# Moving the right operands' pool by 128 bytes and making the last projection's pool a multiple of 256 bytes, in a decoder block on one core

## The chip, the cores and the metric

The kernel runs on one core of one Trainium2 chip. The metric is the device time of one execution in microseconds (us), taken as the median of three runs. A separate execution was recorded by the hardware profiler; its views are quoted here as "the profile" or "the trace". The core has a matrix engine (PE, with its weight loads listed apart as PEld), a vector engine (DVE), a scalar engine (ACT), a general engine (POOL), an engine that mostly issues transfers (SP), and 16 DMA engines. On-chip memory has 128 partitions; an address here is a byte offset inside a partition, the same in all 128.

## The reference, cut to what matters

A residual block over 2048 tokens of width 1024:

```
h    = rms_norm(x, g) * (1 + scale) + shift            # scale, shift, gate from silu(c) @ w_mod
proj = h @ w_in                                        # 1024 x 8192: rnn x, rnn gate, q, k, v, attn gate, 2 merge gates
y_rnn  = (rg_lru(conv(x_rnn)) * silu(z_rnn)) @ w_out_rnn
y_attn = (dilated_attention(rope(q), rope(k), v) * silu(z_attn)) @ w_out_attn
merged = sigmoid(g_r + b) * y_rnn + sigmoid(g_a + b) * y_attn
x    = x + gate * (merged @ w_o);  out = rms_norm(x, g_final)
```

All matrix products keep float32 accuracy. The addresses at which operands lie do not enter the result.

## The kernel before, in words

Every float32 operand is split into a high part and a low part (`hi_act`, `lo_pool`, `lo_dve`, L157 to L168), and `mm3` (L152) makes one product out of three matmuls: high by high, high by low, low by high. Each matmul comes with its own weight load: the left operand (`lhsT`) is loaded into the array and stands, the right operand (`rhs`) moves through it, 512 columns or 256 at a time. The profile writes the result and then the two operands, so `X<-T,S` is a matmul into bank X whose operands lie in tiles T and S.

The stages, in order of time:

1. Values: `value_sums` and `value_runs` make v. Here a T tile (the normalised input, turned) is the standing operand, and an S tile (split weights, 256 columns) moves. For two of the four blocks of tokens half of T's part is held in `b12h` and `b12l` instead. With 4 weight groups, 4 blocks, 2 banks, 2 halves, 8 slices and 3 matmuls there are 1,536 such matmuls, 384 of them with b12.
2. The input projection, once for each half of the tokens. `strassen` (L362) makes 7 products where 8 would be plain; `prod` runs 4 slices times `mm3`, 12 matmuls of 512 columns for each product. Here S stands and T moves. There are 28 pairs of column tiles in each half, so 2 x 28 x 7 x 12 = 4,704 matmuls. Between products the recurrent branch puts in 32 groups of 6 matmuls (`gates` in `recurrent`), whose operands `xh`, `xl`, `gh`, `gl` lie in one pool.
3. Attention, whose operands all lie in one pool, with the two output projections (`steps`, results in pj) spread between its matmuls. Their moving operands `yh` and `yl` lie in pool `fl`, their standing ones in S0 to S3. The last two blocks of the second projection have their moving operand in F tiles: 192 matmuls with F against S0 to S3.
4. The last projection (`output_products`): eight pairs of token tiles, seven products each, 12 matmuls a product, F moving, S standing. Product i of each pair uses Si: B11 takes S0, T2 S1, T3 S2, T1 S3, B21 S4, T4 S5, B22 S6. PE runs them in the order S0, S6 of the pair before, S1, S2, S3, S4, S5.

The order of work inside each engine is written out by hand (`manual_schedule`) from L601 on.

Pools are laid out as two stacks in each partition. The left stack begins with pool `cp` (constants and small vectors, each tile rounded up to 32 bytes), and everything opened on the left lies behind it: `hp` with the 14 T slots, `vx` with b12, `rp` with xh, xl, gh, gl, `ap` with the attention's operands, and `fp` with the F slots. The right stack begins at the top end: `pS` with S0 to S3, `pR`, then `wS` and `wq` with S4 to S6, later `fl` with yh and yl, and for the last projection `gp`, which then holds S4 to S6.

In the program before, `cp` ends at byte 18,528 (72 x 256 + 96). A T or F slot has 8,192 bytes, a slice of it 2,048, so each of these operands starts at 96 modulo 256. S0 to S3 lie from 212,960 (831 x 256 + 224) on, in steps of 4,096 bytes, with slices of 512, so they start at 224 modulo 256; so do S4 to S6 in `wS`, and yh and yl in `fl`. Pool `gp` takes gf 4,096, three S 12,288, four xo 16,384, u1 to u3 8,192, four ss of 16 bytes rounded up to 32 (128), and two jk 2,048: 43,136 bytes, 168 x 256 + 128. It ends at 204,768, where `pR` begins, so it starts at 161,632, 96 modulo 256, and its S4 to S6 stand at 96 too. The pool of xh, xl, gh and gl puts them at 160, b12h and b12l are at 224, and cs (the identity for transposes, in `cp`) is at 128.

| operands (moving against standing) | before, modulo 256 | difference |
|---|---|---|
| T against S, input projection | 96, 224 | 128 |
| yh, yl against S0 to S3 | 224, 224 | 0 |
| F against S0 to S3 | 96, 224 | 128 |
| F against S4 to S6, last projection | 96, 96 | 0 |
| S against T, values | 224, 96 | 128 |
| S against b12, values | 224, 224 | 0 |
| xh, xl against gh, gl | 160, 160 | 0 |

Of the kernel before, what the change touches and what calls it, by code (L numbers as in the profile page):

```python
# [10 lines left out]
F32 = mybir.dt.float32  # L11
# [9 lines left out]
P = 128  # L21
# [68 lines left out]
def decoder_block(ctx, tc, x, c, positions, g_norm, w_mod, b_mod, w_in, b_gate, conv_w, conv_b,  # L90
                  w_a, b_a, w_x, b_x, lam, w_out_rnn, w_out_attn, w_o, g_final, cst, out):
    nc = tc.nc
    cnt = [0]

    def T(pool, shape, dt, tag, **kw):
        cnt[0] += 1
        return pool.tile(shape, dt, tag=tag, name=f"{tag}_{cnt[0]}", **kw)
# [26 lines left out]
    cp = ctx.enter_context(tc.tile_pool(name="cp", bufs=1))  # L124
# [20 lines left out]
    par = T(cp, [P, N_PAR], F32, "par")  # L145
    ones = T(cp, [P, 1], F32, "ones")
    nc.gpsimd.memset(ones[:], 1.0)

    def mm(o, l, r, st, sp, **kw):
        nc.tensor.matmul(o, lhsT=l, rhs=r, start=st, stop=sp, **kw)  # L150
# [1010 lines left out]
    for t in range(6):  # L1161
        pieces = []
        i0 = t * P
        while i0 < (t + 1) * P:
            hd, i = divmod(i0, 96)
# [777 lines left out]
    def output_products(fill):  # L1943
# [120 lines left out]
        def soon(d, fn):  # L2064
            i = max([e[1] for e in jobs], default=0) + 1
            jobs.append((done_n[0] + d, i, fn))
            jobs.sort(key=lambda e: e[:2])
# [24 lines left out]
        squares_of = {}  # L2092

        def first_root(ss):
            nc.vector.tensor_scalar(ss[:, 0], ss[:, 0], ss[:, 3], EPS, ALU.add, ALU.add)
            nc.scalar.activation(ss[:, 1], ss[:, 0], AF.Sqrt)

        def last_root(ss):
            v, y, t = (ss[:, i] for i in range(3))
            nc.vector.reciprocal(y, y)  # L2100
            nc.vector.tensor_scalar(t, y, y, v, ALU.mult, ALU.mult)
            nc.vector.tensor_scalar(t, t, -0.5, 1.5, ALU.mult, ALU.add)
            nc.vector.tensor_scalar(y, y, t, None, ALU.mult)

        def finish_last(x, i, j, ps):

            xo, cols = XO[x, i], slice(j * CH, (j + 1) * CH)
            tt(xo[:, cols], ps[:], xo[:, cols], ALU.add)
            whole = (x, i) in squares_of
            if not whole:  # L2110
                squares_of[x, i] = T(gp, [P, 4, 1], F32, "ss", bufs=4)
            ss = squares_of[x, i]
            jk = T(gp, [P, CH], BF16, "jk", bufs=2)
            nc.scalar.activation(jk[:], xo[:, cols], AF.Square, scale=D ** -0.5, accum_out=ss[:, 3 if whole else 0])
            if (i, j) == (0, 1):
                U[i, j] = T(gp, [P, CH], F32, "u1", bufs=1)[:]
                tt(U[i, j], xo[:, cols], gf[:, cols], ALU.mult)
            else:
                U[i, j] = xo[:, cols]
                nc.gpsimd.tensor_tensor(U[i, j], xo[:, cols], gf[:, cols], ALU.mult)  # L2120
            if whole:
                first_root(ss)
                last_root(ss)
                n, r = order[x]
                for q in (1 - j, j):
                    v = U[i, q]
                    if q == 1 - j:
                        nc.scalar.activation(v, v, AF.Copy, scale=ss[:, 1])
                    elif i:
                        nc.gpsimd.tensor_tensor(v, v, ss[:, 1].broadcast_to([P, CH]), ALU.mult)  # L2130
                    else:
                        nc.vector.tensor_scalar(v, v, ss[:, 1], None, ALU.mult)
                    nc.sync.dma_start(outv[n, r + i][:, q * CH : (q + 1) * CH], v)

        def finish(x, i, j, ps, u):

            if x == len(order) - 1:
                return finish_last(x, i, j, ps)
            xo, cols = XO[x, i], slice(j * CH, (j + 1) * CH)
            tt(xo[:, cols], ps[:], xo[:, cols], ALU.add)  # L2140
            if (x, i) not in squares_of:
                squares_of[x, i] = [T(gp, [P, 4, 1], F32, "ss", bufs=4)]
            ss = squares_of[x, i]
            ss.append(j)
            whole = len(ss) == 3
            n, r = order[x]
            ss = ss[0]

            def square():
                jk = T(gp, [P, CH], BF16, "jk", bufs=2)  # L2150
                nc.scalar.activation(jk[:], xo[:, cols], AF.Square, scale=D ** -0.5, accum_out=ss[:, 3 if whole else 0])

            def scale(q):
                if not q:
                    last_root(ss)
                cq = slice(q * CH, (q + 1) * CH)
                nc.vector.scalar_tensor_tensor(xo[:, cq], xo[:, cq], ss[:, 1], gf[:, cq], ALU.mult, ALU.mult)
                if q:
                    nc.sync.dma_start(outv[n, r + i], xo[:])

            soon(1, square)
            if whole:
                soon(2, lambda: first_root(ss))
                soon(3, lambda: scale(0))
                soon(4, lambda: scale(1))
# [6 lines left out]
        for x in range(len(order)):  # L2172
# [17 lines left out]
            V = T(pj, [P, CH], F32, "pj") if x % 2 else T(pf, [P, CH], F32, "V")  # L2190
            product(V, "T1", True, False, 7 * x + 3)
            finish(x, 1, 1, V, u3)
            product(X, "B21", False, True, 7 * x + 4)
            finish(x, 0, 0, X, None)
            Y = T(pf, [P, CH], F32, "Y")
            product(Y, "T4", True, True, 7 * x + 5)
            finish(x, 1, 0, Y, u3)

            def last(x=x, V=V):
# [77 lines left out]
```

## Time and profile before

| what | before |
|---|---|
| median of 3 runs | 2260.27 us (2259.36 to 2262.28) |
| the profiled execution | 2258.11 us, its span 2256.0 us |
| DMA moved | 520.19 MB, mean 231 GB/s |
| POOL, ACT, DVE busy share of the span | 54%, 57%, 65% |

A span runs from the first instruction to the last; 2.1 us of the profiled execution lie outside of it. Views of stretches list for each stretch the busy time of every engine with the count of its instructions in brackets, then the clock granted to PE and the DMA engines' busy share. Views in order of time merge neighbouring instructions of one kind: the first column is the start of the first, the second the time from there to the end of the last, and "x12" their count. Matmuls overlap in the array, so the time of one (some 395 ns) is not the time it costs; that is the distance from one start to the next, called the step here.

### The profile page before, as it was taken

Reading aid. Unit: us, or ns where it says so; the run is one execution under the profiler, and the core shown is the slowest. Engines: PE = TensorE matmul, PEld = TensorE weight load, DVE = VectorE, ACT = ScalarE, POOL = GpSimd, SP = SyncE. Lnnn points to the kernel's source line nnn. Section 1 sums busy time; section 2 is a strip of 40 time slices with the busy share of each in tenths; the row PEclk is TensorE's granted clock in tenths of the full one; section 3 lists DMA queues with packets and bytes.
Section 4 is the critical chain, followed back from the end, with each engine's and each line's share of the span. In section 5 each row is a group of like instructions: output and inputs, shape, how many; then the busy total and the mean of one; then the engine's idle time right before and its main releaser. Section 6 shows DMA issues by size and latency. Waiting matters only on the chain.

```text
span 2256.0 us, 34354 instructions
## 1 busy us (share of the span) xinstructions
PE 2201.3 (98%) x11359; PEld 1845.6 (82%) x11359; DVE 1456.7 (65%) x2451; ACT 1294.0 (57%) x2560; POOL 1215.1 (54%) x902
## 2 busy tenths in 40 slices
PE   8999999999999999999999999999999999999898
PEld 5998888888877988888888887888989898977786
DVE  5578788778557664555645455467677878645776
ACT  3547767678533436666766611477677887632333
POOL 2277677676556344445445312356565656433786
PEclk9999999999999999999999999999999999999999
DMA  8354665565797647877787899989988888788553
GB/s 283 90 171 165 204 212 179 189 228 189 233 268 230 219 138 224 260 233 237 241 256 237 261 309 296 298 266 289 272 280 264 241 261 257 234 275 260 174 168 131
DMA packets 455433, 520.19 MB, mean 231 GB/s; under 512 B 90360, under 2 KB 333268, under 8 KB 454232
## 3 DMA queue, kind: packets, MB, share of 16 engines
q1 hardware_dynamic: 427492, 434.95, 63.6%
q10 hardware_dynamic: 27572, 83.00, 9.7%
q8 instruction: 90, 1.47, 0.3%
q14 instruction: 87, 0.71, 0.1%
q0 software_dynamic: 192, 0.05, 0.0%
HBM read 340.67 MB, written 177.21 MB: 230 GB/s over the span
## 4 chain that ended last, share of the span: by engine, by line
PE 48%; DMA 10%; DVE 3%; issue 3%; ACT 2%; POOL 2%; SPq 1%; ACTq 0%; POOLq 0%; DVEq 0%
PE X L150 9%; PE pj L150 9%; PE V L150 7%; PE W L150 4%; PE Z L150 4%; PE Y L150 4%; PE sc L150 4%; PE o L150 4%; DMA fg<-mrT 1%; DMA meT<-fg 1%; PE pg L150 1%; PE pT L1628 1%; DMA wo<-in_w_o_dram 1%; PE pT L1641 1%; DMA R<-in_w_in_dram 1%
## 5 line engine op out<-in xcount | busy, mean ns | idle before, releaser
L164 POOL TENSOR_TENSOR S<-R,S 128x512 fp32r<-128x512 f32 x278 | 408.2, 1473 | 402.8 <-ACT S L158 361.4
L150 PE MATMUL X<-T,S 128*128 128x512 f32 x1344 | 334.8, 398 | 10.4 <-ACT S L158 5.2
L150 PE MATMUL V<-T,S 128*128 128x512 f32 x1344 | 331.2, 395 | 0.0
L150 PEld LDWEIGHTS X<-T,S 128*128 128x128 f32 x1344 | 255.0, 190 | 72.1 <-ACT S L158 5.9
L150 PEld LDWEIGHTS V<-T,S 128*128 128x128 f32 x1344 | 252.3, 188 | 58.3 <-DVE ev L466 0.3
L150 PE MATMUL pj<-yh,S 128*128 128x512 f32 x848 | 287.8, 397 | 4.6 <-DMA S<-wD 3.9
L158 ACT ACTIVATE S<-R 128x512 fp32r<-128x512 f32 x278 | 170.7, 622 | 134.5 <-DMA R<-in_w_in_dram 111.8
L164 POOL TENSOR_TENSOR S<-s,S 128x512 fp32r<-128x512 f32 x108 | 165.9, 1537 | 128.7 <-ACT S L158 97.0
L150 PEld LDWEIGHTS pj<-yh,S 128*128 128x128 f32 x848 | 160.9, 190 | 37.9 <-DVE fg L1859 4.3
L1544 ACT ACTIVATE pp<-pp,st 128x256 f32<-128x256 f32 (+3 forms) x256 | 133.4, 523 | 75.2 <-DVE st L1543 74.8
L150 PE MATMUL pj<-yl,S 128*128 128x512 f32 x424 | 167.5, 395 | 2.1 <-DVE yl L167 1.2
L150 PE MATMUL Y<-T,S 128*128 128x512 f32 x672 | 165.5, 395 | 0.0
L150 PE MATMUL Z<-T,S 128*128 128x512 f32 x672 | 165.4, 395 | 0.0
L150 PE MATMUL W<-T,S 128*128 128x512 f32 x672 | 165.3, 395 | 0.0
L150 PEld LDWEIGHTS Z<-T,S 128*128 128x128 f32 x672 | 126.6, 188 | 29.7
L150 PEld LDWEIGHTS Y<-T,S 128*128 128x128 f32 x672 | 126.6, 188 | 29.3
L150 PEld LDWEIGHTS W<-T,S 128*128 128x128 f32 x672 | 126.4, 188 | 29.3
L158 ACT ACTIVATE S<-s 128x512 fp32r<-128x512 f32 x108 | 67.3, 623 | 109.7 <-DVE s L290 35.1
L167 DVE TENSOR_TENSOR ptl<-pT,pth 128x384 fp32r<-128x384 f32 (+1 forms) x160 | 97.8, 628 | 49.3 <-ACT pth L158 47.1
L960 DVE SCALAR_TENSOR_TENSOR xc<-xr,par,xc 128x512 f32<-128x512 f32 x96 | 96.6, 1006 | 50.2 <-ACT xc L954 48.0
L1543 DVE CUSTOM_DVE_ANT_0 pp<-sc,msk 128x256 f32<-128x256 f32 (+3 forms) x256 | 104.2, 449 | 37.2 <-PE sc L150 35.0
L164 POOL TENSOR_TENSOR kq<-kraw,kq 128x512 fp32r<-128x512 f32 (+1 forms) x64 | 101.3, 1593 | 41.7 <-ACT kq L158 41.7
(382 smaller groups left out, 4841.6 us busy)
## 6 DMA issues: line engine op xcount, KB each, us to landing
sD<-S ACTq DMA_DIRECT2D x118, 512.0 KB, 3.7
S<-sD SPq DMA_DIRECT2D x118, 512.0 KB, 5.1
S<-wD SPq DMA_DIRECT2D x100, 512.0 KB, 5.7
R<-in_w_in_dram SPq DMA_DIRECT2D x196, 256.0 KB, 4.1
wD<-s ACTq DMA_DIRECT2D x64, 256.0 KB, 4.9
T<-in_w_mod_dram SPq DMA_DIRECT2D x8, 1024.0 KB, 12.0
vN<-ev SPq DMA_DIRECT2D x64, 128.0 KB, 2.8
zaT<-ev SPq DMA_DIRECT2D x32, 256.0 KB, 2.8
```

What stands on the lines that cost most here:

```text
L150: nc.tensor.matmul(o, lhsT=l, rhs=r, start=st, stop=sp, **kw)
L158: nc.scalar.activation(o, i, AF.Copy)
L164: nc.gpsimd.tensor_tensor(o, i, h.bitcast(F32), ALU.subtract)
L167: nc.vector.tensor_tensor(o, i, h.bitcast(F32), ALU.subtract)
L960: nc.vector.scalar_tensor_tensor(xc, xr[:, i : i + CH], cw(i), xc, ALU.mult, ALU.add)
L1543: nc.vector.tensor_tensor_reduce(pdst, s_ps, mask, 1.0, 3e38, ALU.add, ALU.min, m_)
L1544: nc.scalar.activation(pdst, pdst, AF.Exp, bias=m_, scale=-1.0, accum_out=l_)
L1628: nc.tensor.transpose(pt[:, c0 + j * P : c0 + (j + 1) * P], pp[i][:, k * P : (k + 1) * P], ident)
L1641: nc.tensor.transpose(pt[:, c * P : (c + 1) * P], pp[:, half * P : (half + 1) * P], ident)
```

## The change

A tile `align` of 32 floats (128 bytes) is added at the end of the group of tiles `cs`, `par`, `ones` in pool `cp`, and POOL sets it to zero once. All later tiles of `cp` and all pools on the left stack move up by 128 bytes: T, F, b12, xh, xl, gh, gl and the attention's operands. The four `ss` tiles of pool `gp` grow from 16 to 256 bytes each, of which the first four columns are used as before. `gp` then has 43,136 + 896 = 44,032 bytes (172 x 256), begins at 160,736, and its S4 to S6 start at 224 modulo 256. T and F are then at 224 as well, b12 at 96, xh, xl, gh and gl at 32. No instruction of the engines beside that one memset is added, removed or reordered in the source.

```
     ones = T(cp, [P, 1], F32, "ones")
     nc.gpsimd.memset(ones[:], 1.0)
+    align = T(cp, [P, 32], F32, "align")
+    nc.gpsimd.memset(align[:], 0.0)
...
             if not whole:
-                squares_of[x, i] = T(gp, [P, 4, 1], F32, "ss", bufs=4)
+                squares_of[x, i] = T(gp, [P, 64, 1], F32, "ss", bufs=4)
...
             if (x, i) not in squares_of:
-                squares_of[x, i] = [T(gp, [P, 4, 1], F32, "ss", bufs=4)]
+                squares_of[x, i] = [T(gp, [P, 64, 1], F32, "ss", bufs=4)]
```

## Prediction before the run

> **What bounds the kernel now.** I read the page first, then the stretches, then PE's instructions in order of time. The page gives the span and the share of each engine.
>
> ```profile
> span 2256.0 us, 34354 instructions
> ...
> PE 2201.3 (98%) x11359; PEld 1845.6 (82%) x11359; DVE 1456.7 (65%) x2451; ACT 1294.0 (57%) x2560; POOL 1215.1 (54%) x902
> ```
>
> PE has work in hand for 98% of the span. What can change is the step from one matmul to the next. The view of four stretches (two of the input projection, its end, the last projection) says where PE is alone the bound:
>
> ```profile
> core 0: us, PE busy (x) PEld busy (x) DVE busy (x) ACT busy (x) POOL busy (x), PEclk, DMA share, GB/s
> 160.00:640.00 480.00, 475.65 (x2051) 385.07 (x2050) 356.13 (x383) 324.59 (x521) 325.58 (x217) 1.00 0.62 204
> 845.00:1360.00 515.00, 515.00 (x2227) 417.69 (x2226) 263.91 (x337) 301.36 (x468) 216.14 (x161) 1.00 0.79 251
> 1360.00:1420.00 60.00, 57.19 (x236) 44.90 (x235) 29.04 (x43) 11.57 (x20) 13.64 (x11) 0.97 0.97 304
> 2130.00:2256.00 126.00, 117.92 (x512) 95.95 (x510) 85.92 (x156) 47.46 (x114) 93.30 (x63) 0.98 0.47 151
> ```
>
> In the second row PE never rests: 515.0 us for 2,227 matmuls, 231 ns each. Time there is the number of matmuls times their step. The granted clock is 1.00 in the dense stretches, so nothing can be gained by warming PE, and the other engines have a quarter of the time or more to spare there. The shape of the work in the input projection is seen in order of time (starts in the first column, twelve matmuls a product):
>
> ```profile
> 403.50 0.39 PE L150 MATMUL pg<-xh,gh 128*128 128x512 f32 x1
> ...
> 403.96 0.40 PE L150 MATMUL pg<-xh,gl 128*128 128x512 f32 x1
> 404.20 0.39 PE L150 MATMUL pg<-xh,gh 128*128 128x512 f32 x1
> ...
> 404.89 2.94 PE L150 MATMUL V<-T,S 128*128 128x512 f32 x12
> 407.67 2.96 PE L150 MATMUL X<-T,S 128*128 128x512 f32 x12
> ...
> 424.41 0.85 PE L150 MATMUL V<-T,S 128*128 128x512 f32 x3
> ```
>
> From 407.67 to 424.41 six products start, 72 matmuls: 16.74 us, a step of **232.5 ns**, operands 128 apart modulo 256 (the table of addresses above). The last projection has both kinds of address in the same seven products:
>
> ```profile
> 2173.13 2.95 PE L150 MATMUL Z<-F,S 128*128 128x512 f32 x12
> 2175.93 2.95 PE L150 MATMUL W<-F,S 128*128 128x512 f32 x12
> 2178.72 2.95 PE L150 MATMUL V<-F,S 128*128 128x512 f32 x12
> 2181.50 2.88 PE L150 MATMUL X<-F,S 128*128 128x512 f32 x12
> 2184.22 2.89 PE L150 MATMUL Y<-F,S 128*128 128x512 f32 x12
> 2186.95 2.96 PE L150 MATMUL X<-F,S 128*128 128x512 f32 x12
> 2189.74 2.92 PE L150 MATMUL V<-F,S 128*128 128x512 f32 x12
> 2192.50 2.95 PE L150 MATMUL Z<-F,S 128*128 128x512 f32 x12
> ```
>
> Z and W (S1, S2, 128 apart) take 5.59 us for 24 matmuls, 232.9 ns. X and Y behind them (S4, S5, congruent) take 5.45 us for 24, 227.1 ns. X after that (S0, 128 apart) has 2.79 us for 12 again, 232.5. Shape, engine, clock and moving pool are the same in all; the standing operand's address is what differs. It is not the name of the tile: in the input projection S4 to S6 stand at 224 and the six products quoted, which use six of the seven S tiles, all step by about 232. The V at 2189.74 (S6, congruent, right after a product that is not) takes 2.76 us, **230.0** a step: congruence needs some matmuls to take hold. Nor is it the place 96: the first output projection runs at 224 against 224.
>
> ```profile
> 1418.22 0.62 PE L150 MATMUL pj<-yh,S 128*128 128x512 f32 x2
> ...
> 1422.98 0.62 PE L150 MATMUL pj<-yh,S 128*128 128x512 f32 x2
> ```
>
> Seven groups of three (two yh, one yl) from 1418.22 to 1422.98: 4.76 us for 21, **226.7 ns**. This is the undisturbed step of congruent operands at the very remainder that the change gives to T and F.
>
> **The change part by part.**
>
> *T against S, 4,704 matmuls.* They go from 232.5 to 226.7: 4,704 x 5.8 ns = 27.3 us. The bound from above is this; from below it is 230.0, the V after a break, with 4,704 x 2.5 = 11.8 us. I take 226.7, because product follows product here without a change of remainder, as X and Y do, and those keep their step across the change of bank.
>
> *Breaks.* 32 groups of xh, xl against gh, gl stand between products. Their own operands move together and stay congruent: from 403.50 to 404.89 six matmuls, 231.7 a step, unchanged. After each the next product pays the 230.0 of the V: 32 x 12 x 3.3 ns = 1.3 us lost again.
>
> *F against S0 to S3 in the last projection.* 8 pairs x 4 products x 12 = 384 matmuls from 232.8 (24 in 5.59 us) to 226.7: 2.3 us, and S6 without its break 8 x 12 x 3.3 ns = 0.3 us. The first pair is stopped by other work (a wait of 4.2 us for POOL's split, below), so seven eighths: 2.3 us.
>
> *F against S0 to S3 before it.* 192 matmuls x 6.1 = 1.2 us at most. They run where PE waits for others, between 2010 and 2130; I count nothing, with 0 and 1.2 as bounds.
>
> *S against T, values (256 columns).* These become congruent, and b12 stops being so. Both kinds are in the trace:
>
> ```profile
> 120.98 1.59 PE L150 MATMUL X<-S,T 128*128 128x256 f32 x12
> ...
> 125.25 0.40 PE L150 MATMUL Z<-S,b12h 128*128 128x256 f32 x2
> ...
> 131.01 1.58 PE L150 MATMUL Z<-S,T 128*128 128x256 f32 x12
> ```
>
> 128 apart, 36 matmuls in 4.27 us, 118.6 ns; congruent, 48 from 125.25 to 131.01 in 5.76 us, 120.0 ns. So congruence costs 1.4 ns at this width: 1,152 of T lose and 384 of b12 win, (1,152 - 384) x 1.4 = **1.1 us lost**. This part goes against the change.
>
> *What stays.* yh and yl against S0 to S3, and the attention's operands among each other, keep their differences. The memset runs on POOL before its first transfers; the rows before it and after:
>
> ```profile
> 0.74 0.10 POOL L147 MEMSET ones<- 128x1 f32 x1 [0.29 <-POOLq L2263]
> ...
> 4.02 0.51 POOL L619 DMA_DIRECT2D prow<-in_lam_dram  x1
> ...
> 14.55 0.27 PE L663 MATMUL pg<-cs,prow 120*128 120x120 f32 x1
> ```
>
> A memset of one column takes 0.10 us; 32 columns may take several times that, while six loads of prow are queued behind it on POOL. The last is issued by 4.53 and used at 14.55, behind PE's warming matmuls: some 10 us of cover for it. Without the cover the memset would cost its own length. The larger ss tiles change no instruction; they move gp's tiles by 896 bytes over what fl had held, so a first load into them may wait for another former user. The two longest waits of PE are these:
>
> ```profile
> PE X L150 <- ACT S L158: 5.2, 2, 4.9
> PE X L150 <- POOL S L164: 4.8, 2, 4.2
> ```
>
> The second is the start of the last projection. I take 0 for the move, with 1 us more or less as an estimate of a quarter of that wait.
>
> *Where the gain could be lost.* Faster products ask earlier for S tiles. In 845 to 1360 the DMA engines are at 0.79 and would go to 0.81; between 1360 and 1420 they are at 0.97, and PE already waits. So I give up the gain of the 205 or so matmuls of T there, 205 x 5.8 = 1.2 us. In 160 to 640 DVE is busiest, 356 of 480 us, and would go from 74% to 76%.
>
> *The sum.* 27.3 - 1.3 + 2.3 - 1.1 - 1.2 = **26.0 us less**. The span goes from 2256.0 to 2230.0; with 2.1 us outside it the profiled execution goes from 2258.1 to 2232.1. The median shown, 2260.27, is 2.2 above that execution, so I forecast 2260.3 - 26.0 = **2234 us** for the median. Its own range is 2228 (nothing lost to breaks, transfers or values, F's 1.2 won) to 2240 (step of 227.9, a fifth of the T gain lost).
>
> **The rivals.**
>
> *Each product has to take hold anew: 2247.* If every change of S tile or bank is a break, all T and F matmuls stay at 230.0: 11.8 + 384 x 2.8 ns = 12.9 us, less 1.1 for the values, gives 2248.5; the same 2247 or so comes out if the second half of the input projection, 2,352 matmuls, turns out to be held by transfers and keeps its time (13.6 of the 27.3 us lost). For it: the V row at 230.0, and DMA at 0.79. Against: Y's 2.73 us right behind X's 2.72, and a stretch of 515 us without one wait.
>
> *The addresses don't matter: 2260.* Then S4 and S5 step faster for another reason, say fewer neighbours on DVE or POOL at that point of the pair, and the shift does nothing; less the 1.1 us of the values it is 2261. Against it: 226.7 appears in two stages with different neighbours, each time with congruent operands, and in none of the quoted rows without. The Trainium skill speaks for this rival: "TensorE: Matmul & The Clock Gate", Part 2 (What happens when you issue a matmul), says that PE reads the moving operand and the next weights through two independent ports, so that loading weights takes nothing from a running matmul. By that rule the sum is zero. The trace here does not agree: 232.9 against 227.1 in neighbouring products.
>
> *Congruent operands get in each other's way in the dense stage: 2300.* Just after a break a congruent step can be long: 403.96 to 404.20 is 240 ns for one matmul of the group. If T and S in the input projection fall into that phase and hold it, 4,704 x 7.5 ns = 35 us are added, with F's 384 x 7.2 = 2.8 and the values' 1.1 it is 2299. It decides where the step goes over 232.5. Against it: the six matmuls of that group average 231.7, and where congruent matmuls follow one another for longer, every row quoted settles under 227.2.
>
> **How the numbers follow.** The forecast has 0.81, the 2247 case 0.11, no effect 0.04, the slower case 0.04. Range 2228 to 2248: it takes in the forecast's own range and most of the second case. A measurement of this kernel can tell about 0.2%, 4.5 us, from no change; the first two cases are faster than that: 0.92 faster, 0.04 the same, 0.04 slower.
>
> **What would show it.** In the changed trace six products of T,S should start within 16.3 to 16.4 us instead of 16.74; Z, W, X, Y of the last projection should all have starts 2.72 apart; S,T in the values should go from 118.6 to 120 ns and b12 the other way; xh,gh groups should stay near 231.7. The sum of PE's waits should stay as it is. The prediction is wrong if T's step stays over 230, if it falls but PE's waits for S or for transfers grow by as much, or if the start of the last projection moves by more than 2 us.

## The result, and the profile after

| what | before | after |
|---|---|---|
| median (runs) | 2260.27 us (5, 2259.27 to 2262.32) | 2250.71 us (5, 2247.24 to 2254.49) |
| profiled execution, its span | 2258.11, 2256.0 | 2250.71, 2248.6 |

The ratio of after to before is 0.9952, with a 95% interval of 0.994 to 0.9963: faster by 9.6 us, where 26 were forecast. The page of the changed kernel begins so:

```profile
span 2248.6 us, 34354 instructions
...
PE 2183.3 (97%) x11358; PEld 1847.6 (82%) x11359; DVE 1462.8 (65%) x2451; ACT 1292.7 (57%) x2560; POOL 1216.4 (54%) x903
```

PE has 18.0 us less of busy time, yet the span is 7.4 us shorter. So the steps fell, and more than half of what they saved has become waiting. The same four stretches as before, in the changed kernel:

```profile
core 0: us, PE busy (x) PEld busy (x) DVE busy (x) ACT busy (x) POOL busy (x), PEclk, DMA share, GB/s
160.00:640.00 480.00, 471.65 (x2074) 386.79 (x2073) 358.71 (x387) 324.62 (x522) 328.15 (x218) 1.00 0.63 207
845.00:1360.00 515.00, 511.56 (x2256) 421.96 (x2255) 273.02 (x344) 302.01 (x470) 219.34 (x163) 1.00 0.81 256
1360.00:1420.00 60.00, 56.53 (x238) 45.61 (x237) 27.16 (x39) 11.95 (x21) 14.17 (x11) 0.96 0.94 298
2130.00:2256.00 126.00, 110.57 (x488) 91.22 (x486) 82.01 (x150) 43.76 (x105) 88.39 (x59) 0.97 0.44 139
```

In the first row PE starts 2,074 matmuls, 23 more than before (1.1%), though each one costs 2.5% less. PE, which had rested 4.3 us of these 480, now rests 8.4. (The last row reaches past this kernel's end.) Where PE now waits, by the view of waits, is seen stage by stage. This is PE in the first half of the input projection, from 145 to 735, in the kernel before:

```profile
PE X L150 <- ACT u L399: 4.3, 1, 4.3
PE pg L525 <- DVE t L545: 3.0, 1, 3.0
```

and in the changed one (us in total, times, longest):

```profile
PE X L152 <- ACT u L401: 4.3, 3, 3.5
PE pg L527 <- DVE t L547: 3.9, 1, 3.9
PE pg L152 <- POOL xl L166: 3.1, 3, 2.1
PE V L152 <- DVE t L468: 2.3, 2, 1.6
PE V L152 <- DVE ev L468: 1.0, 2, 0.7
PE V L152 <- ACT S L160: 0.2, 1, 0.2
```

7.3 us have become 14.8, and the new ones have three different engines as releasers.

The lengths of the stages, read from the starts of their first and last matmuls in each trace, say where the two profiled executions differ (7.4 us of span; the medians differ by 9.6). The column "forecast" is the prediction's sum, divided by stages.

| stage, us | before | after | moved | forecast |
|---|---|---|---|---|
| first half of the input projection | 582.4 | 581.4 | -1.0 | -13.0 |
| second values | 103.5 | 103.5 | 0.0 | +0.5 |
| second half of the input projection | 574.2 | 566.4 | -7.8 | -11.8 |
| attention, to the first X<-F | 672.7 | 671.8 | -0.9 | 0 |
| last projection, from there | 165.9 | 168.0 | +2.1 | -2.3 |

### The profile page after: what moved, and what is told of

Read it like the earlier page. It is cut to its first block, busy times and chain, and to the rows that moved or that the text cites. A ratio compares the mean times of both kernels' runs of the same rounds, so it can differ in the third digit from the quotient of the medians.

```text
span 2248.6 us, 34354 instructions
## 1 busy us (share of the span) xinstructions
PE 2183.3 (97%) x11358; PEld 1847.6 (82%) x11359; DVE 1462.8 (65%) x2451; ACT 1292.7 (57%) x2560; POOL 1216.4 (54%) x903
## 4 chain that ended last, share of the span: by engine, by line
PE 53%; DMA 7%; DVE 3%; issue 2%; ACT 2%; POOL 2%; SPq 1%; ACTq 0%; POOLq 0%; DVEq 0%
PE pj L152 11%; PE X L152 9%; PE V L152 7%; PE W L152 5%; PE Z L152 5%; PE o L152 4%; PE sc L152 4%; PE Y L152 4%; PE pT L1630 1%; DMA R<-yaT 1%; PE pg L152 1%; DMA wo<-in_w_o_dram 1%; PE pT L1643 1%; DMA meT<-fg 1%; DMA oD<-s 1%
## 5 line engine op out<-in xcount | busy, mean ns | idle before, releaser
L152 PE MATMUL V<-T,S 128*128 128x512 f32 x1344 | 325.8, 391 | 3.9 <-DVE t L468 2.7
```

## The experiments

All are edits of the changed kernel, unless "before" is named. Line numbers are up to 2 higher than in the kernel before.

### Which address does it

`align_only` keeps the align tile and leaves the ss tiles at 4 columns. `gp_only` has the ss tiles of 64 and no align tile. `shift256` moves everything by 256 bytes in place of 128, with ss at 4:

```
-    align = T(cp, [P, 32], F32, "align")
+    align = T(cp, [P, 64], F32, "align")
```

> The 128 bytes in cp alone, gp as before. Theory A (the step did fall to 226.7 ns, and the gain was eaten by waits for engines and transfers that keep their own pace): T against S steps at 227 as in the changed kernel; in the last projection S0 to S3 are congruent, S4 to S6 are not (232.7), so 8 x 36 matmuls x 6 ns = 1.7 us more than the changed kernel, about 2252 us. Theory B (gp's larger ss tiles, which move its tiles over what fl held, cost the 4 us lost at the start of the last projection): 2248 or less, and the wait of 4.7 us for S before Z there is gone.

> The larger ss tiles alone, no 128 bytes in cp. T against S as before, 232.5 ns a step; in the last projection F is at 96 and all S at 224, nothing congruent, so 288 matmuls lose 6 ns. A: before plus 1.7 us, about 2262, start of the last projection as before. B: 4 us more on top, about 2266.

> 256 bytes in cp instead of 128, gp as before: all left pools move, every remainder stays. A, and congruence as the cause of the step: T steps at 232.5, time as before within 0.2% (2256 to 2264). Rival (the move itself changes waits or transfers, whatever the remainder): over 2264, with waits of POOL's xl in the first half or of S at the start of the last projection.

Measured: `align_only` 2251.36 us, 0.9961 [0.9943, 0.9979]; `gp_only` 2262.92, 1.0014 [1.0005, 1.0023]; `shift256` 2261.54, 0.9999 [0.9988, 1.0009]. A shift by a whole 256 bytes gives nothing, one by 128 gives all of it, and what counts is not that something was moved. The last projection of `align_only`, with S0 to S3 at the remainder of F and S4 to S6 128 away (S4 and S5 are the first X and Y below), shows it in one pair, in order of time:

```profile
2165.37 2.91 PE L152 MATMUL Z<-F,S 128*128 128x512 f32 x12
2168.12 2.88 PE L152 MATMUL W<-F,S 128*128 128x512 f32 x12
2170.84 2.89 PE L152 MATMUL V<-F,S 128*128 128x512 f32 x12
2173.57 2.95 PE L152 MATMUL X<-F,S 128*128 128x512 f32 x12
2176.36 2.96 PE L152 MATMUL Y<-F,S 128*128 128x512 f32 x12
2179.16 2.90 PE L152 MATMUL X<-F,S 128*128 128x512 f32 x12
```

W takes 2.72 us to the next start and V 2.73; X and Y take 2.79 and 2.80. It is the trace of before with the roles exchanged. The move of gp alone costs 1.1 to 5.2 us by its interval: it takes the congruence from S4 to S6 and gives none, and the products of its last projection start 2.80 us apart; with the align tile it makes no difference that the medians of `align_only` and the changed kernel (2251.36 and 2250.71) can show. The rival of a cost in gp's larger tiles falls: `align_only` has tiles of the old size, and its wait for ACT's S before Z, at the start of the last projection, is 5.0 us.

### The same kernel again

`after_again` has no edit.

> The changed kernel itself, profiled once more. If the losses at the ends of the stages belong to the program (theory A), PE's lead over the kernel before falls at the same places by about as much: some 3 us near 690 to 745, 4 near 1330 to 1410, 4 near 2070 to 2120. If they are chance of the transfers (rival), they move or change by several us, and the first half of the input projection, which has no such stretch, still gains nothing.

2249.08 us, a single execution. First half 580.5, second half 566.6, last projection 168.2. To see where the gain went I set the start of every instruction against the start of the same instruction in the kernel before; the difference is called the lead. In both executions of the changed kernel PE's lead grows evenly and is lost at the same places: in the first half, where it falls by 3.3 us in the first trace and 3.2 in this one from 350 to 460; at that half's end, 690 to 745 (4.3 and 2.8); between 1330 and 1372 (3.4 and 3.6); and at the start of the last projection, 2071 to 2121 (3.9 and 4.1).

The first of these losses belongs to the program: it is 3.2 to 3.3 us in all five traces that have the new step and an unedited first half (these two, `align_only` and the two kernels built on the changed one in the section on the end of the second half). For the lengths of stages two traces are too few. With the old step, the first half takes 578.5 to 582.4 us in the five traces that leave it unedited; with the new step, 578.1 to 581.4 in five. One execution differs from the next by up to 4 us there, and no gain of the change shows at all. The last projection takes 165.9 to 169.2 us in five traces with the old addresses (`gp_only` is not among them) and 164.8 to 168.2 in five with the new ones (without `align_only`), so the 2.1 us of the table are not shown to be the change's.

### Who sets the pace of the first half

In the traces of before and after, the lead of PE in the first half goes from 0.8 us at 200 to 4.1 at 350. Those of DVE, ACT and POOL stay at 0.3 to 0.4 from 215 to 375. They did not speed up with PE; PE ran ahead of them until it met its next input. `two_of_three` tests that by taking a third of the projection's matmuls away (of each slice's three products only high by high stays, and low by low takes the place of the two mixed ones):

```
-                mm3(ps[:], s[:, 0, k, :], s[:, 1, k, :], bh[:, k, :], bl[:, k, :],
-                    first=first and k == 0, last=last and k == KH - 1, skip_group_check=True)
+                mm(ps[:], s[:, 0, k, :], bh[:, k, :], first and k == 0, False, skip_group_check=True)
+                mm(ps[:], s[:, 1, k, :], bl[:, k, :], False, last and k == KH - 1, skip_group_check=True)
```

> On the changed kernel: both halves of the input projection leave out one of the three matmuls of each slice and pair high with high and low with low (two of the three terms are gone), so PE has a third less there: 2352 x 0.227 = 533 us a half becomes 356. All other engines' work stays. A: the first half (before 574 us from its first product to the end of its last) is held by ACT, DVE and POOL at their own pace and gets shorter by less than 10%; the second half, which has less work beside it, by over 20%. Rival (the other engines follow PE and only a few late operations cost): both halves shorten alike, by near a third.

2175.84 us, a single execution like the three that follow. PE has 784 matmuls, 784 x 226.7 ns = 178 us, less to do in each half. The first half shrinks by 9.9 us, to 571.5; the second by 66, to 500.1. The first 240 us of the first half's dense part, in the kernel before:

```profile
160.00:400.00 240.00, 240.00 (x1035) 194.64 (x1034) 192.76 (x205) 169.47 (x274) 171.05 (x113) 1.00 0.57 192
```

and in `two_of_three`:

```profile
160.00:400.00 240.00, 186.48 (x700) 139.34 (x700) 191.43 (x204) 170.50 (x276) 172.51 (x115) 0.91 0.58 194
845.00:1100.00 255.00, 225.56 (x905) 178.35 (x904) 169.95 (x201) 198.13 (x312) 145.53 (x106) 0.93 0.90 285
1100.00:1300.00 200.00, 160.49 (x633) 124.08 (x633) 115.80 (x147) 93.16 (x149) 75.93 (x56) 0.91 0.93 297
```

This pair of rows is the core of the case. In the kernel before, PE is busy for all of the 240 us and DVE for 80% of it. With a third of PE's projection work gone, DVE, ACT and POOL get through 204, 276 and 115 instructions in the same 240 us, as against 205, 274 and 113. The first half is paced by them, though none is busy for more than 80%. In the second half, where S comes split from memory, the DMA share rises to 0.90 and 0.93 instead; that transfers set the floor of 500 us there is the likely reading, which this run alone does not show. PE's longest waits in the first half of `two_of_three` name all three engines:

```profile
PE pg L152 <- POOL xl L166: 27.6, 15, 3.8
PE X L152 <- ACT u L401: 18.5, 9, 5.4
PE V L152 <- DVE ev L468: 16.5, 13, 5.3
PE pg L152 <- ACT xh L160: 16.1, 12, 2.4
```

Three runs lighten one link each, on top of `two_of_three`. `pool_light` leaves out POOL's multiply of zs by sg, `dve_light` two of the three `taps`, and `act_light` replaces the square root, before each of which the trace has a table load of 1.28 us, by a copy:

```
-                (2, lambda: nc.gpsimd.tensor_tensor(z[:], z[:], sg[0][:], ALU.mult))))
+                ))
...
-                for i in range(1, 4):
+                for i in range(1, 2):
...
-                nc.scalar.activation(t, t, AF.Sqrt)
+                nc.scalar.activation(t, t, AF.Copy)
```

> On the kernel with two of three matmuls: POOL's multiplication of zs by sg is left out (16 a half, 1.3 to 1.75 us each, some 27 us of POOL in the first half). If POOL sets the pace of the first half, its 571.5 us fall by about as much, 20 us or more; if another engine does, by less than 8.

> On the kernel with two of three matmuls: two of DVE's three convolution taps are left out (32 a half, about 1 us each, some 33 us of DVE in the first half). If DVE sets the pace (it is busiest there, 80%), the first half falls by 20 us or more from 571.5; if another does, by less than 8.

> On the kernel with two of three matmuls: the square root on ACT is replaced by a copy, so 16 loads of its function table a half go (1.28 us each, 20.5 us, and some that load the next table back). If ACT sets the pace, the first half falls by 15 us or more from 571.5; if another does, by less than 8. If all three engines are links of one chain, each of the three light kernels gains a part.

2168.92, 2183.09 and 2179.58 us; first halves 559.2, 567.0 and 566.6. Against 571.5 that is 12.3 us for some 25 us taken from POOL, 4.5 for some 36 from DVE, 4.9 for some 38 of ACT (30 table loads fewer). No engine gives back what was taken from it, which agrees with a chain over three engines in which POOL counts most. The gains from DVE and ACT are single executions and hardly larger than the 4 us by which executions of one kernel differed above, so that these two are links isn't shown by their size.

### Relieving POOL with all three matmuls

If that chain holds the first half, lightening it should give PE's shorter step its worth. The multiply is moved to DVE in the changed kernel (`mult_dve_after`) and in the one before (`mult_dve_before`):

```
-                (2, lambda: nc.gpsimd.tensor_tensor(z[:], z[:], sg[0][:], ALU.mult))))
+                (2, lambda: nc.vector.tensor_tensor(z[:], z[:], sg[0][:], ALU.mult))))
```

> The changed kernel with the multiply of zs by sg (16 in a half, 1.57 us each on POOL) moved to DVE, where the like multiply t by gi takes 1.05 us. Theory A (the first half of the input projection is held by the chain of DVE, ACT and POOL, with POOL the strongest link): in the runs with two of three matmuls 27 us less on POOL gave 12.3 us and 33 us less on DVE gave 4.5, so 17 us more on DVE cost 2.3 and the chain gains about 10; with all three matmuls PE's own floor of the half is 2,352 x 226.7 ns + 96 x 231 = 555 us, and the half should go from 581 to about 573, the median from 2251 to about 2243. Rival B (the first half loses its gain to something else, PE's own order or transfers): the half stays within 2 us of 581 and the median within 3 us of 2251. Rival C (DVE, the busiest, is the link that decides): the half gets longer, 583 or more, and the median is 2253 or more.

> The same move of the multiply in the kernel before, whose steps are 232.5 ns. Theory A: PE's own floor of the first half is 569 us there, so less of the chain's relief can be used: from 582 to about 577, median 2260 to about 2255; and the difference between the two kernels in the first half grows from 1 us to 4 or more. Rival B: the half stays at 582 and the difference at 1 to 2 us. Rival C: 584 or more.

| | first half | median | ratio to before |
|---|---|---|---|
| before | 582.4 us | 2260.18 us | |
| `mult_dve_before` | 579.5 | 2261.08 | 1.0004 [0.9993, 1.0015] |
| `mult_dve_after` | 576.7 | 2245.69 | 0.9939 [0.992, 0.9958] |

The direction is theory A's, the size about half: 4.7 us less in the changed kernel where 8 were expected. That 576.7 lies 1.4 us under the lowest of the five unedited halves with the new step (578.1). The 2.9 us in the other kernel show nothing, since unedited halves with the old step go down to 578.5; so the growth of the difference from 1.0 to 2.8 us, where 4 were expected, isn't shown either.

What settles it is the place. Between 330 and 460 PE waits 2.6 to 3.1 us for POOL's xl in all five traces with the new step and POOL's multiply, and not once in the five with the old step. In `mult_dve_after` no wait for POOL is left from 180 to 700:

```profile
PE X L152 <- ACT u L401: 4.3, 2, 3.6
PE V L152 <- DVE t L468: 0.8, 1, 0.8
PE V L152 <- DVE xr L468: 0.5, 1, 0.5
PE V L152 <- DVE ev L468: 0.2, 1, 0.2
```

PE's lead there grows by 0.9 us from 350 to 460, where it falls by 3.2 or 3.3 in the five. Rivals B and C fall for the changed kernel, but the chain is only loosened. PE is busier in the same stretch than it was in the changed kernel (474.84 against 471.65), and DVE too:

```profile
160.00:640.00 480.00, 474.84 (x2084) 390.09 (x2083) 368.02 (x408) 329.75 (x530) 305.44 (x205) 1.00 0.65 210
```

In the kernel before the same edit brings nothing in the end: its lead of 2.8 us over the unedited kernel is 2.6 at 1300, 1.1 at 1400 and 0.1 at the end. `mult_dve_after` has the lowest median of the kernels that leave nothing out, but its interval overlaps that of the changed kernel, so that it beats it isn't shown.

### Moving the gates

The waits for `xl` sit at the gate matmuls. `gates6` puts these one product later, `gates6_mult` does that and moves the multiply as well:

```
-    GATES = 5
+    GATES = 6
```

> The changed kernel with the gate matmuls of the recurrent branch, and all that follows them, put one product later (GATES 6 in place of 5): PE reaches them 2.7 us later, so its waits for POOL's xl there (3.1 us in three waits between 330 and 460) should be gone. Theory A (the engines keep their own pace over the half): PE gets no work out of it, it is late at S, ev or u next; the half stays within 2 us of 581 and the median within 3 of 2251. Rival D (the loss is only the place of the gates in PE's order): the half shrinks by 4 us or more, to 577 or below, and the median to 2247 or below.

> Both edits in the changed kernel: the multiply on DVE and the gates one product later. Theory A: as with the multiply alone, within 3 us of it, about 2243, half about 573. Rival D: as with the gates alone or better by its 4 us. If neither edit helps, 2251 or more.

2288.47 us, 1.0126 [1.0106, 1.0146], and 2279.46, 1.0092 [1.0074, 1.011]; first halves 612.9 and 604.8. Both theories missed it by more than 30 us. The wait for xl is gone, but the whole recurrent branch behind the gates now meets other work in the queues of DVE, ACT and POOL. In the first 480 us of the dense part they get less done (372 DVE instructions in place of 387), and PE waits from 180 to 700 for what they make:

```profile
PE V L152 <- DVE ev L468: 8.7, 6, 3.5
PE X L152 <- ACT u L401: 8.1, 5, 2.7
PE V L152 <- DVE xr L468: 7.2, 3, 3.4
```

That agrees with the chain as the bound, since PE's own work is unchanged, but theory A as I had put it ("within 2 us") took the pace of these engines for a fixed number. It hangs on the order in which their work is queued. With the multiply moved too, the half is 8.0 us shorter again. Which meeting costs most was not tried.

### The end of the second half

In the second half the leads of all engines grow together, PE's to 10.9 us at 1320, and 4.1 of it go between 1340 and 1420. In the changed kernel ACT stands there waiting for raw weights, and PE for ACT's S:

```profile
1356.24 0.63 ACT L160 ACTIVATE S<-R 128x512 fp32r<-128x512 f32 x1 [17.37 <-DMA R<-in_w_in_dram]
...
1356.93 0.73 PE L152 MATMUL X<-T,S 128*128 128x512 f32 x2 [2.37 <-ACT S L160]
1358.34 4.14 PE L152 MATMUL X<-T,S 128*128 128x512 f32 x10 [0.68 <-POOL S L166]
```

To tell transfers from the tail's own chain, the eight loads of w_o towards the end of that half (0.5 MB each, for weights of the last projection) are left out. `tail_light_after` and `tail_light_before` let ACT copy the gate in their place:

```
-                    rows = slice((i * KH + k) * P, (i * KH + k + 1) * P)
-                    nc.sync.dma_start(v[i][:], w_o[0, rows, :].rearrange("p (j c) -> p j c", j=2))
+                    nc.scalar.activation(v[i][:].rearrange("p j c -> p (j c)"), gate_b[:], AF.Copy)
```

> The changed kernel without the eight loads of w_o (0.5 MB each) at the end of the second half; ACT copies the gate into their tiles instead, so that the last projection's weights are other numbers. Six of these loads lie between 1320 and 1415 in the trace of before, where the DMA engines are at 0.90 to 0.98. Theory T (the 4.1 us of lead that PE loses between 1340 and 1420 go to transfers): 4.2 MB at the 290 GB/s of that stretch are 14 us of transfer time less, so the loss goes away and the second half takes 562 to 563 us in place of 566.4, the median about 2247. Rival U (PE is held there by the tail's own chain of DVE and ACT): the second half stays within 1 us of 566, the median at 2251.

> The same loads left out of the kernel before. Theory T: PE is slower there and is held less; the second half goes from 574.2 to 572 to 574, and the difference between the kernels in this half grows from 7.8 us to 10 or more, towards the 12.7 that 2,352 steps of 5.8 ns less the breaks and the gates' own steps give. Rival U: 574 and a difference of 8.

2250.45 us (0.9957 [0.9938, 0.9977]) and 2262.76 (1.0012 [0.9999, 1.0024]); second halves 566.4 and 579.1. The difference grew to 12.7 us, but both kernels got a new wait of my making. ACT's copy waits 10.32 us for the gate's load, and PE then 4.57 for the u that is queued behind it on ACT:

```profile
1288.08 2.00 ACT L1313 ACTIVATE wo<-gb 128x1024 f32<-128x1024 f32 x2 [10.32 <-DMA gb<-gateD]
...
1291.14 4.62 PE L152 MATMUL X<-T,S 128*128 128x512 f32 x12 [4.57 <-ACT u L401]
```

Inconclusive, so the pair was made again with a memset on POOL in the copy's place (`tail_memset_after`, `tail_memset_before`):

```
+                    nc.gpsimd.memset(v[i][:], 1.0)
```

> The changed kernel with the eight loads of w_o left out as before, but with a memset on POOL (10 of 40 us busy there) in their place: ACT's copy had to wait 10.3 us for the gate's own load and cost PE 4.6 us at 1291. Theory T (transfers hold the tail): that wait and PE's waits for S at 1357 (2.4 and 0.7 us) are both gone, the second half takes 562 us, and the median is 2246 to 2247. Rival U (the tail's own chain): PE still waits 2 us or more for S, u or t between 1300 and 1395, the half stays at 566 and the median at 2251.

> The same in the kernel before. Theory T: 573 to 575 us in the second half, and a difference of 11 to 13 us between the two kernels there in place of 7.8. Rival U: 574 and a difference of 8.

2246.62 us (0.994 [0.9898, 0.9982]) and 2258.95 (0.9989 [0.9976, 1.0002]). The second half takes 560.6 us in the changed kernel (566.4 with the loads) and 573.2 in the other (574.2): a difference of **12.6 us** in place of 7.8. With all loads, the second halves of four kernels with the old step lie between 574.2 and 576.8, those of four with the new one at 563.9 (`align_only`), 566.4, 566.6 and 566.7. So 560.6 is 3.3 us under the lowest of its kind, and 573.2 only 1.0. In the changed kernel without the loads PE has no rest from 1250 to 1390, and the DMA share from 1300 on, 0.88 to 0.93 in the changed kernel with them, has come down to 0.83 and 0.85:

```profile
1250.00:1300.00 50.00, 50.00 (x223) 41.37 (x222) 21.27 (x27) 21.63 (x32) 16.07 (x13) 1.00 0.95 298
1300.00:1340.00 40.00, 40.00 (x178) 33.14 (x177) 24.20 (x34) 6.97 (x12) 12.39 (x9) 1.00 0.83 255
1340.00:1390.00 50.00, 50.00 (x223) 41.39 (x222) 28.85 (x41) 6.45 (x11) 14.69 (x12) 1.00 0.85 246
```

Theory T holds for the changed kernel: these transfers hold PE in the tail. In the kernel before, the 1.0 us are within what executions differ by. The medians don't show it by themselves, since the interval of the changed kernel without the loads takes in that of the one with them.

## Why the prediction was wrong, point by point

**The step: right.** T against S went to 226.7 ns. In the changed kernel, four products from 408.56 to 419.44 are 48 matmuls in 10.88 us:

```profile
401.34 0.50 PE L152 MATMUL pg<-xl,gh 128*128 128x512 f32 x1 [0.35 <-POOL xl L166]
...
408.56 2.88 PE L152 MATMUL Y<-T,S 128*128 128x512 f32 x12
...
419.44 2.88 PE L152 MATMUL W<-T,S 128*128 128x512 f32 x12
423.06 2.32 PE L152 MATMUL V<-T,S 128*128 128x512 f32 x9 [0.74 <-DVE ev L468]
```

W to V takes 3.62 us in place of 2.72: its wait of 0.74, and PE's next steps are slower for a moment. Such places are where the gain of the steps around them went.

**Breaks: right.** The product after a group of gates takes 2.74 to 2.75 us in 31 of 32 places (2.78 before), up to 0.03 more than the others, so at most 1.0 us in all where 1.3 was forecast. The groups themselves stay at 1.38 us where no wait falls into them (29 of 32).

**Values: right.** S against T went up to 120.0 ns, b12 down to 118.5, as in these rows: 36 matmuls from 119.90 to 124.22, 48 from 114.21 to 119.90. The second values stage as a whole stayed at 103.5 us, where 0.5 more were forecast.

```profile
114.21 0.39 PE L152 MATMUL V<-S,b12h 128*128 128x256 f32 x2
...
119.90 1.60 PE L152 MATMUL V<-S,T 128*128 128x256 f32 x12
...
124.22 1.60 PE L152 MATMUL X<-S,T 128*128 128x256 f32 x12
```

**Last projection: the step right, its start missed.** All seven products of a pair now start 2.72 us apart, S6's too:

```profile
2166.97 2.88 PE L152 MATMUL Z<-F,S 128*128 128x512 f32 x12
...
2183.29 2.88 PE L152 MATMUL V<-F,S 128*128 128x512 f32 x12
2186.01 2.88 PE L152 MATMUL Z<-F,S 128*128 128x512 f32 x12
```

From 2121 to the end PE's lead grows by some 2.1 us, where the prediction had 2.3. But between 2071 and 2121 it had lost some 4, which the prediction had in no term. PE's waits between 2000 and 2125 in the changed kernel begin:

```profile
PE Z L152 <- ACT S L160: 4.7, 1, 4.7
PE X L152 <- POOL S L166: 4.2, 1, 4.2
```

The 4.2 is that of before; the 4.7 is new, and the two waits for fg of before (1.5 and 1.2) are gone. That is 2.0 us more waiting. About as much again lies in the steps behind the new stop: the granted clock is 0.50 from 2080 to 2084, and the twelve matmuls of Z take 5.26 us from start to start in place of 2.72:

```profile
2079.80 5.46 PE L152 MATMUL Z<-F,S 128*128 128x512 f32 x12 [4.70 <-ACT S L160]
2085.06 3.12 PE L152 MATMUL W<-F,S 128*128 128x512 f32 x12
```

After the two waits for fg the clock had stayed at 1.00. The leads of the other engines were already falling from 8.2 to 5.3 between 1990 and 2050. Here fg is stored as meT and read back before ACT can split it. That the time of these transfers is what doesn't shrink is my reading of the trace; no run tested it. Nor is the wait bound to the shorter step: `shift256`, with the old one, waits 2.9 us for ACT's S at the same place, and `mult_dve_after` not at all. As the prediction's own mark had it, a start of the last projection moved by more than 2 us speaks against its sum.

**The step that failed: 27.3 us counted as if PE alone set the time of both halves.** The prediction read "PE never rests" as "PE is the bound" and DVE's 74% as "a quarter of the time or more to spare". It took 13.0 us from the first half for granted, and 1.0 came in this pair of traces, nothing over all of them. `two_of_three` shows why: the work of DVE, ACT and POOL holds the half at 571.5 us even with a third of PE's projection matmuls gone, and PE at the new step needs 2,352 x 226.7 + 96 x 231 ns = 555 us by itself. At the old step that was 569 us: the two were level, so PE could be at 100% and no longer worth speeding up. "The sum of PE's waits should stay as it is" failed with it. It is 7.3 against 14.8 us in this half, and 3.1 to 7.4 against 10.5 to 14.8 over the five traces of each kind. Besides, steps of T,S are slower behind such stops: those over 0.25 us, without a wait, cost 4.3 us over the half in place of 2.6, and 6.9 in `after_again`.

**Lost to transfers: right mechanism, too small.** 1.2 us were given up for one stretch of 60 us. Taking the loads of w_o away shortened the half by 5.8 us in the changed kernel and by 1.0 in the one before, so by these traces the change lost 4.8 us there; by the means of the four traces of each kind it is 2.9. The prediction gave up only the gain made inside the stretch; a stretch with a floor also takes back gain brought into it from earlier.

**The rivals.** The case of 2247 had the second half held by transfers and the first one free. It was the other way round: the first half keeps its time and the second gives most of its gain. That 2250.71 came out near its 2247 is chance. The other form of that case, steps that stay at 230.0, fell with the 226.7. "The addresses don't matter" fell with `shift256` and `align_only`. The Trainium skill, "TensorE: Matmul & The Clock Gate", Part 2 (What happens when you issue a matmul), says that loading the next weights takes no read bandwidth from a running matmul. By that, where the two operands lie to each other should not count; the traces don't agree, with 2.79 against 2.72 us for twelve matmuls. What in the chip makes the difference no run shows. Congruent operands did not get in each other's way at 512 columns.

**The range.** Its lower end was added up wrong: 2260.3 less 27.3, 2.3 and 1.2 us is 2229.5 and not 2228. It doesn't bear on the outcome, which lies above the upper end.

**What stays open.** Which link of the chain, or which order of its work, would bring the first half down to PE's 555 us; why PE loses another 1.4 to 4.3 us at that half's end in the traces with the new step; and the start of the last projection.

## What to carry to other kernels

Before a cheaper step of the busiest engine is credited with its full worth, look for what the other engines would do if that engine were free: the kernel with a third of PE's projection work left out answers in one run, where busy shares of 74% and 100% misled. An engine at 100% may stand level with a chain of engines each at 70 to 80%, and a chain's pace lies in its order and its waits, not in its shares. Where a stage ends in a stretch with a floor of its own (the transfers at 0.9 and more), count against the change all the lead that arrives there, not only what is gained inside.

## What the runs showed of the hardware

For these f32 matmuls of 128 x 512, each with its own weight load, the step is 226.7 to 227.1 ns where moving and standing operand start at the same remainder modulo 256 bytes and 232.5 to 233.3 where they start 128 apart. Which remainder it is made no difference in the two tried (96 before, 224 after), a shift by 256 changes nothing, and the sign turns at 256 columns: 120.0 congruent against 118.6 or 118.5. Other distances than 0 and 128 were not tried. After a stop of PE one of its next steps took 306 to 339 ns in place of 227, at each of five stops between 376 and 425 in the changed kernel. A longer stop can cost more than its own length: behind the one of 3.92 us that ends at 718 the granted clock is 0.50 from 719 to 722.5, and twelve matmuls take 4.87 us in place of 2.72. It is not fixed by the length alone: after a stop of 2.1 us at 380 the clock stayed at 1.00 in one execution of the changed kernel and fell to 0.57 in the other.
